# The first weight matrix of a two-layer encoder, loaded raw and split on the engines chunk by chunk

## The chip, the cores and the metric

The kernel runs on one core of one Trainium2 chip. The metric is device time in microseconds (us) for one execution of the whole program. Engines are named as in the profile: PE is TensorE (PEld its weight loads), DVE is VectorE, ACT is ScalarE, POOL is GpSimd, SP is SyncE.

## The reference

Two layers of an encoder work on x of 512 tokens by 1024 features, all in float32. Each layer does

```
h = rms_norm(x, attn_norm_g[l]);  z = h @ w_in[l]
qa, ka, va, qb, kb, vb, ga, gb = split(z)          # 512,128,128,512,512,512,1024,1024 columns
ya = window_gqa(rope(norm(qa)), rope(norm(ka)), va, sink_a[l]) @ w_proj_a[l]
yb = neighbourhood_attn(norm(qb), norm(kb), vb, rel_bias_b[l]) @ w_proj_b[l]
x = x + (sigmoid(ga) * ya + sigmoid(gb) * yb) @ w_out[l]
h = rms_norm(x, ffn_norm_g[l])
x = x + (silu(h @ w_gate[l]) * (h @ w_up[l])) @ w_down[l]
```

The case is about the very first product, the 512 columns of qa in layer 0.

## The kernel before

**Precision.** A float32 product is made of three products in the faster float32r format: each operand is split into a high part (its rounding to float32r) and a low part (what is left). For a weight the high part H is a transfer that rounds on its way, and the low part L is made by `w_low`: ScalarE writes -H, and an accumulating transfer adds the weight from memory a second time. Both transfers are issued by GpSimd, and the second has to wait for ScalarE.

**Slabs.** Weights come in slabs. The first matrix (columns of qa) has four slabs of 256 rows by 512 columns, 512 KB each; a slab holds two chunks of 128 rows. `w_load(i)` issues the transfer of H of slab i, `w_low(i)` makes L, and `w_take` hands them to the product. For later slabs both are issued at due times ahead of their use.

**The first product.** `token_matmul` keeps four PSUM banks, one for each block of 128 tokens. For each of eight chunks k it does twelve products of 128 by 512: for each block xh·H, xh·L, xl·H. In layer 0 the chunks of x are prepared on the way by `start(nrm, k, second)`: PE transposes the chunk `xin[k]` in four blocks, ACT writes its high part `xh` with the norm's gain, DVE copies the transposed chunk to `xT`, then DVE makes the low part `xl`, ACT squares the chunk, and DVE adds the squares up in `acc`. Two chunks are prepared ahead of the first product, the other six between products. After the eighth chunk four small products with `ones` sum the squares over the features, DVE computes the reciprocal root (`rstd`) in some sixteen tiny operations, and PE turns it into rows; only then does the program's next matrix (columns of ka and va) begin.

**The order.** PE's main line is written out in code order. Everything beside it (the rope tables in `chain_tables`, heads, splits) stands in generators, and a dry run with a planner's costs decides once, at build time, between which products their instructions go. On the chip each engine then runs its list in that order. Buffers lie in two arenas (float32 and float32r), and a packer gives them addresses from the uses in the dry run.

**Small loads.** SP issues x in eight chunks, the identity matrix and the norm gains `vec`. POOL issues the first three slabs, the rest of the constants, four loads of norm vectors, `posi`, two loads `gqa`, and the sinks `snk`. A transfer may have to wait for an earlier one of its kind: GpSimd's ninth waits until its first has landed.

Of the kernel before, what the change touches and what calls it, by code (L numbers as in the profile page):

```python
# [12 lines left out]
F32 = mybir.dt.float32  # L13
F32R = mybir.dt.float32r
I32 = mybir.dt.int32
AF = mybir.ActivationFunctionType
ALU = mybir.AluOpType
AX = mybir.AxisListType

P = 128  # L20
# [4 lines left out]
NB = S // P  # L25
KD = D // P
# [64 lines left out]
def by_columns(ap):  # L91

    return ap.rearrange("p (r cc c) -> p cc r c", cc=NB, r=8)


def held(ap):
    return ap.rearrange("p (cc r c) -> p cc r c", cc=NB, r=8)
# [116 lines left out]
def trunk(ctx: ExitStack, tc: tile.TileContext, a: dict, out: bass.AP, lay: Layout):  # L214
    nc = tc.nc
    PS = bass.MemoryType.PSUM
    cp = ctx.enter_context(tc.tile_pool(name="cp", bufs=1))
# [37 lines left out]
    def at_bank():  # L255
        return pa.tile([P, S], F32, tag="at", name=nm("at"))
# [76 lines left out]
    T = Engine(nc.tensor, "pe")  # L333
# [167 lines left out]

    highs, lows, used = {}, {}, [0]

    def w_load(i):

        if i not in highs:
            n1, n2, src = plan[i]
            highs[i] = buf([n1, n2], F32R)
            for at, ap in src:
                n = ap.shape[1]  # L510
                GQ.dma_start(highs[i][:, :, at : at + n], ap.rearrange("(k p) n -> p k n", p=P))

    def w_low(i):

        if i not in lows:
            n1, n2, src = plan[i]
            lows[i] = buf([n1, n2], F32R)
            A.activation(lows[i], highs[i].bitcast(F32), AF.Copy, scale=-1.0)
            for at, ap in src:
                n = ap.shape[1]  # L520
                GQ.dma_start(
                    lows[i][:, :, at : at + n], ap.rearrange("(k p) n -> p k n", p=P), accum_op=ALU.add
                )
# [110 lines left out]
    G.memset(vec2, 0.0)  # L634
    G.memset(ones, 1.0)
    G.memset(magic, 0x5F3759DF)
    warm = cp.tile([P, 2], F32, tag="warm", name="warm")
    A.copy(warm, ones)
    xv = a["x"].rearrange("o (b p) d -> p (o b) d", p=P)
    xin = []  # L640

    def x_load(c):
        t = act().rearrange("p (b n) -> p b n", b=NB)
        Q.dma_start(t, xv[:, :, P * c : P * c + P])
        xin.append(t)


    x_load(0)
    Q.dma_start(ident, a["consts"][:, :P])
    for i, n in enumerate(("attn_norm_g", "ffn_norm_g")):  # L650
        Q.dma_start(vec[16 * i : 16 * i + 16], a[n].rearrange("l (k p) -> (l k) p", p=P))
    w_load(0)
    for c in range(1, KD):
        x_load(c)
        if c in (3, 5):
            w_load((0, 3, 5).index(c))
    GQ.dma_start(cst[:, P:], a["consts"][:, P:])
    for i, n in enumerate(("q_norm_b", "k_norm_b")):
        for h in range(2):
# [7 lines left out]
        GQ.dma_start(gqa[:, i], a[n].rearrange("l d -> (l d)").unsqueeze(0).to_broadcast([P, DEPTH * HD]))  # L667
    snk = cp.tile([P, DEPTH, 8], F32, tag="snk", name="snk")
    GQ.dma_start(snk, a["sink_a"].rearrange("l h -> (l h)").unsqueeze(0).to_broadcast([P, DEPTH * 8]))
    ps = at_bank()  # L670
    T.transpose(ps[:, :32], vec, ident[:32, :32])
    V.tensor_copy(vecT, ps[:, :32])

    def gain(norm, k):
        c = 16 * (norm % 2) + 8 * (norm // 2) + k
        return vecT[:, c : c + 1]
# [140 lines left out]
    def token_matmul(nrm, evac, begin=None):  # L817

        ps = [mm_bank() for _ in range(NB)]
        if begin is not None:  # L820
            begin(0, False)
            w_low(0)
            begin(0, True)
            begin(1, False)
            begin(1, True)
            tick(0.0)
        for k0 in range(0, KD, 2):
            wk = w_take()
            order = [(b, k) for b in range(NB) for k in range(2)]
            if begin is not None:  # L830
                order.sort(key=lambda x: x[1])
            for i, (b, k) in enumerate(order):
                t = slice(P * b, P * b + P)
                kk = k0 + k
                hi, lo = wk[k]
                mm(ps[b], nrm.xh[kk][:, t], hi, kk == 0, False)
                mm(ps[b], nrm.xh[kk][:, t], lo, False, False)
                mm(ps[b], nrm.xl[kk][:, t], hi, False, kk == KD - 1)
                tick(UNIT)
                if kk == KD - 1:  # L840
                    evac(b, ps[b])
                if begin is not None and i in (0, 2, 4, 6) and k0 < KD - 2:
                    begin(k0 + 2 + i // 4, i % 4 == 2)
                yield UNIT


# [219 lines left out]

    norms = {}

    def start(nrm, k, second):

        if not second:
            ps = at_bank()
            for b in range(NB):
                T.transpose(ps[:, P * b : P * b + P], xin[k][:, b, :], ident)
            A.activation(held(nrm.xh[k]), by_columns(ps), AF.Copy, scale=gain(0, k))
            V.tensor_copy(held(xT[k]), by_columns(ps))
            return
        V.scalar_tensor_tensor(nrm.xl[k], xT[k], gain(0, k), nrm.xh[k].bitcast(F32), ALU.mult, ALU.subtract)
        sq = act()
        A.activation(sq, xT[k], AF.Square)  # L1080
        if nrm.acc is not None:
            V.tensor_tensor(sq, sq, nrm.acc, ALU.add)
        nrm.acc = sq
        if k == KD - 1:
            done.add("acc0")
# [507 lines left out]
```

## Time and profile before

| | us |
|---|---|
| median of 3 runs | 1441.97 |
| lowest and highest of them | 1440.86, 1449.07 |
| the profiled execution | 1444.73 |
| its span (first to last instruction) | 1442.9 |
| PE busy, in the span | 1394.6 (97%) |
| DVE busy | 912.2 (63%) |
| ACT busy | 706.8 (49%) |
| POOL busy (its transfer issues count) | 363.4 (25%) |

In rows of the timeline the first number is the start and the second the duration, both in us; behind them stand engine, line, operation, what it writes and reads, and in brackets how long the engine sat idle ahead of it and for whom. Line 308 is the helper that records every operation, so rows are told apart by names and shapes: `mm` and `at` are PSUM banks, `arena` all buffers of the two arenas. The profiled execution is 1.83 us longer than its span.

### The profile page before, as it was taken

The page shows a single profiled execution, that of the slowest core. Times are in us where ns is not written, and L with a number is a line of the kernel's source. Part 1 is how long each engine was busy: PE and PEld are TensorE (multiplying, and loading weights), DVE is VectorE, ACT ScalarE, POOL GpSimd, SP SyncE. Part 2 cuts the span into 40 slices and gives each one's busy share as a digit, 9 for nine tenths or more (in the row PEclk, how much of TensorE's full clock was granted, in tenths as well). Part 3 has the DMA queues.
Part 4 walks back from the last instruction along what each step waited for, and adds up shares of the span by engine and source line. Part 5 has one row for each costly group of instructions (what it writes and reads, how often), then busy time and mean ns, then how long its engine had stood idle before and what let it go on. Part 6 is the DMA issues. An engine that isn't in the chain of part 4 may idle for free.

```text
span 1442.9 us, 20988 instructions
## 1 busy us (share of the span) xinstructions
PE 1394.6 (97%) x8074; PEld 1224.6 (85%) x8074; DVE 912.2 (63%) x1752; ACT 706.8 (49%) x1191; POOL 363.4 (25%) x370
## 2 busy tenths in 40 slices
PE   5999999999989999999999999999998999999998
PEld 3778888888779999999987788888887999999997
DVE  3977777543667565665648768783448666574753
ACT  3476766643454343433544776574346343343431
POOL 4533222233221111101244322223232120111110
PEclk9999999999999999999999999999998999999999
DMA  9977788799865645645699678888996674736555
GB/s 226 170 159 129 140 161 157 142 196 259 146 139 144 156 117 143 155 112 117 134 201 174 132 129 155 160 158 155 260 206 109 147 175 116 178 89 145 121 100 117
DMA packets 209316, 221.10 MB, mean 153 GB/s; under 512 B 25900, under 2 KB 177632, under 8 KB 209216
## 3 DMA queue, kind: packets, MB, share of 16 engines
q0 software_dynamic: 157808, 165.13, 61.3%
q1 hardware_dynamic: 51408, 54.62, 13.3%
q8 instruction: 64, 1.05, 0.3%
q14 instruction: 36, 0.29, 0.1%
HBM read 207.13 MB, written 2.10 MB: 145 GB/s over the span
## 4 chain that ended last, share of the span: by engine, by line
PE 77%; DVE 12%; issue 3%; DMA 3%; ACT 3%; POOL 1%; DVEq 0%; POOLq 0%; ACTq 0%
PE mm L308 60%; PE at L308 18%; DVE arena L308 9%; ACT arena L308 3%; DVE sm L308 3%; DMA arena<-in_w_in 2%; DMA arena<-in_w_up 1%; POOL arena L308 1%; DMA cst<-in_consts 1%; DVE hf L308 0%; DVE den L308 0%; ACT L308 0%; ACT mm L308 0%; ACT sm L308 0%; DVEq L308 0%
## 5 line engine op out<-in xcount | busy, mean ns | idle before, releaser
L308 PE MATMUL mm<-arena 128*128 128x512 f32 (+1 forms) x5568 | 1123.6, 357 | 20.7 <-ACT mm L308 12.5
L308 PEld LDWEIGHTS mm<-arena 128*128 128x128 f32 x5568 | 907.1, 191 | 150.3 <-ACT mm L308 12.9
L308 ACT ACTIVATE arena<-arena 128x1024 fp32r<-128x1024 f32 (+3 forms) x276 | 232.7, 862 | 188.8 <-DMA arena<-in_w_down 58.9
L308 ACT CAST arena<-arena 128x1024 fp32r<-128x1024 f32 (+2 forms) x250 | 212.0, 864 | 220.9 <-DVE arena L308 218.5
L308 PE MATMUL at<-arena 128*128 128x256 f32 (+2 forms) x1952 | 303.8, 296 | 5.0 <-DVE arena L308 3.5
L308 PEld LDWEIGHTS at<-arena 128*128 128x128 f32 x1952 | 265.7, 191 | 25.9 <-DVE arena L308 8.1
L308 DVE TENSOR_TENSOR arena<-arena,arena 128x1024 fp32r<-128x1024 f32 (+2 forms) x240 | 233.0, 984 | 59.7 <-ACT arena L308 59.3
L308 DVE TENSOR_TENSOR arena<-arena,mm 128x512 f32<-128x512 f32 x144 | 98.7, 686 | 248.4 <-PE mm L308 248.3
L308 POOL DMA_DIRECT2D arena<-in_w_in x168 | 168.3, 1368 | 339.3 <-ACT arena L308 329.5
L308 POOL DMA_DIRECT2D arena<-in_w_down x96 | 98.2, 1218 | 502.1 <-ACT arena L308 357.5
L308 DVE TENSOR_TENSOR arena<-arena 128x1024 f32<-128x1024 f32 (+3 forms) x196 | 158.3, 823 | 4.0 <-ACT arena L308 1.5
L308 DVE TENSOR_TENSOR arena<-at,arena 128x384 fp32r<-128x384 f32 (+4 forms) x206 | 114.4, 562 | 49.6 <-ACT arena L308 42.2
L308 ACT CAST arena<-at 128x384 fp32r<-128x384 f32 (+2 forms) x164 | 74.4, 459 | 117.2 <-PE at L308 99.9
L308 PE MATMUL at<-cst,arena 128*128 128x128 f32 x504 | 85.9, 277 | 9.7 <-DVE arena L308 5.7
L308 PEld LDWEIGHTS at<-cst,arena 128*128 128x128 f32 x504 | 64.3, 142 | 26.8 <-DVE arena L308 6.8
L308 ACT ACTIVATE arena<-arena,negm 128x256 f32<-128x256 f32 (+1 forms) x128 | 71.4, 559 | 6.5 <-DVE negm L308 5.7
L308 DVE TENSOR_TENSOR arena<-mm,arena 128x512 f32<-128x512 f32 x72 | 49.3, 686 | 33.7 <-PE mm L308 33.6
L308 ACT COPY arena<-at 64x512 f32<-64x512 f32 (+1 forms) x60 | 34.9, 582 | 69.8 <-PE at L308 68.5
L308 POOL DMA_DIRECT2D arena<-in_w_out x32 | 35.1, 1287 | 60.5 <-ACT arena L308 60.5
L308 DVE CUSTOM_DVE_ANT_0 arena<-at,cst,nsnk 128x256 f32<-128x256 f32 (+1 forms) x64 | 34.4, 546 | 18.0 <-PE at L308 17.7
L308 DVE CUSTOM_DVE_ANT_0 arena<-at,arena 128x256 f32<-128x256 f32 (+1 forms) x64 | 30.7, 484 | 15.0 <-PE at L308 14.6
L308 DVE TENSOR_SCALAR arena<-arena,sm 128x384 f32<-128x384 f32 (+1 forms) x102 | 33.9, 387 | 1.1
(70 smaller groups left out, 436.4 us busy)
## 6 DMA issues: line engine op xcount, KB each, us to landing
arena<-in_w_in POOLq DMA_DIRECT2D x104, 512.0 KB, 7.2
arena<-in_w_down POOLq DMA_DIRECT2D x80, 512.0 KB, 6.7
arena<-in_w_gate SPq DMA_DIRECT2D x20, 1024.0 KB, 7.5
arena<-in_w_up SPq DMA_DIRECT2D x20, 1024.0 KB, 5.3
arena<-in_w_in POOLq DMA_DIRECT2D x64, 256.0 KB, 6.3
arena<-in_w_out POOLq DMA_DIRECT2D x32, 512.0 KB, 8.4
arena<-in_w_proj_a POOLq DMA_DIRECT2D x16, 512.0 KB, 7.0
arena<-in_w_proj_b POOLq DMA_DIRECT2D x16, 512.0 KB, 5.9
```

What stands on the lines that cost most here:

```text
L308: f(*args, **kw)
```

## The change

The first matrix isn't loaded as rounded high parts any more. `first_load(i)` brings each of its four slabs as plain float32 into a new buffer `raws[i]`: slab 0 in two halves of 256 KB by ACT's queue, slabs 1 to 3 by POOL's. `first_parts(k)` makes the parts of chunk k: ACT casts to the high part, DVE subtracts for the low part. `start(nrm, k)` now does all of a chunk in one go, `first_parts` first, and the copy to `xT` goes from DVE to ACT. One chunk is prepared ahead of the first product instead of two; each further chunk is prepared behind the first three products of the chunk before. The two gain loads go to ACT's queue, ahead of the half slabs; the identity is SP's first load, then x. The `warm` operation, which brings the first table load with it, stands behind the loads.

```
+    def first_load(i):
+        n1, n2, ((_, ap),) = plan[i]
+        raws[i] = buf([n1, n2])
+        ap = ap.rearrange("(k p) n -> p k n", p=P)
+        if i:
+            GQ.dma_start(raws[i], ap)
+        else:
+            for k in range(2):
+                AQ.dma_start(raws[i][:, k], ap[:, k])
+        highs[i], lows[i] = buf([n1, n2], F32R), buf([n1, n2], F32R)
+    def first_parts(k):
+        raw, h, lo = raws[k // 2][:, k % 2], highs[k // 2][:, k % 2], lows[k // 2][:, k % 2]
+        A.copy(h, raw)
+        V.tensor_tensor(lo, raw, h.bitcast(F32), ALU.subtract)
...
-    x_load(0)
     Q.dma_start(ident, a["consts"][:, :P])
...
-        Q.dma_start(vec[16 * i : 16 * i + 16], a[n].rearrange("l (k p) -> (l k) p", p=P))
-    w_load(0)
-    for c in range(1, KD):
+        AQ.dma_start(vec[16 * i : 16 * i + 16], a[n].rearrange("l (k p) -> (l k) p", p=P))
+    for c in range(KD):
         x_load(c)
-        if c in (3, 5):
-            w_load((0, 3, 5).index(c))
+        if c % 2 == 0:
+            first_load(c // 2)
...
         if begin is not None:
-            begin(0, False)
-            w_low(0)
-            begin(0, True)
-            begin(1, False)
-            begin(1, True)
+            begin(0)
             tick(0.0)
...
-                if begin is not None and i in (0, 2, 4, 6) and k0 < KD - 2:
-                    begin(k0 + 2 + i // 4, i % 4 == 2)
+                if begin is not None and b == 0 and kk + 1 < KD:
+                    begin(kk + 1)
...
-    def start(nrm, k, second):
+    def start(nrm, k):
+        first_parts(k)
...
-            V.tensor_copy(held(xT[k]), by_columns(ps))
+        A.copy(held(xT[k]), by_columns(ps))
```

Since the dry run sees other costs at the start, the planner also puts the rope tables elsewhere. Behind the first matrix's part of the program the engines' lists are the same instructions in the same order as before, but for a few rows; buffers have other addresses, and some of the later waits name another engine.

Three places show it. The first is ScalarE in the second half of the first product. Before, around the table load (`trig` are the rope tables, the row of 128x1024 is the -H of a later slab, 128x512 into arena_73 from `at` is xh, 128x512 within arena_72 is the square):

```order
L308 ACTIVATE arena_72<-arena_72 128x512
L308 ACTIVATE arena_73<-at_257,vecT 128x512
L308 ACTIVATE arena_73<-arena_73 128x1024
L308 ACTIVATE arena_72<-arena_72 128x512
L308 ACTIVATE arena_73<-at_287,vecT 128x512
L308 ACT_TABLE_LOAD
L308 ACTIVATE trig<-arena_72 128x128
L308 ACTIVATE arena_72<-arena_72 128x512
L308 ACTIVATE trig<-arena_72 128x128
```

And now, from the -H ahead of chunk 4 to the -H behind chunk 5:

```order
L308 ACTIVATE arena_73<-arena_73 128x1024
L308 CAST arena_73<-arena_72 128x512
L308 ACTIVATE arena_73<-at_232,vecT 128x512
L308 COPY arena_72<-at_232 128x512
L308 ACTIVATE arena_72<-arena_72 128x512
L308 ACT_TABLE_LOAD
L308 ACTIVATE trig<-arena_72 128x128
L308 CAST arena_73<-arena_72 128x512
L308 ACTIVATE arena_73<-at_264,vecT 128x512
L308 COPY arena_72<-at_264 128x512
L308 ACTIVATE arena_72<-arena_72 128x512
L308 ACTIVATE arena_73<-arena_73 128x1024
```

A chunk now has four operations of ScalarE where it had two, and the table load with a `trig` stands between two chunks, ahead of the cast that the next chunk's first products need.

The second place is VectorE, where `chain_tables` begins. Before, it stood behind the copy of chunk 5:

```order
L308 COPY arena_72<-at_223 128x512
L308 CAST vec_76<-posi 4x128
L308 TENSOR_SCALAR nsnk<-snk 128x16
L308 SCALAR_TENSOR_TENSOR arena_73<-arena_72,vecT,arena_73 128x512
L308 TENSOR_TENSOR arena_72<-arena_72 128x512
```

Now it stands behind the sum of squares of chunk 1, ahead of both low parts of chunk 2 (the row with two sources is the weight's, the one with `vecT` is xl):

```order
L308 TENSOR_TENSOR arena_72<-arena_72 128x512
L308 CAST vec_76<-posi 4x128
L308 TENSOR_SCALAR nsnk<-snk 128x16
L308 TENSOR_TENSOR arena_73<-arena_72,arena_73 128x512
L308 SCALAR_TENSOR_TENSOR arena_73<-arena_72,vecT,arena_73 128x512
```

The two small rows that need the loads `posi` and `snk` moved from chunk 5 to chunk 2.

The third place is PE at the end of the first product. Before:

```order
L308 MATMUL mm_120<-arena_73 128x512 x3
L308 MATMUL at_337<-ones,arena_72 128x1 x4
L308 MATMUL mm_121<-arena_73 128x512 x3
L308 MATMUL mm_118<-arena_73 128x512 x3
L308 MATMUL mm_119<-arena_73 128x512 x3
L308 MATMUL mm_120<-arena_73 128x512 x3
L308 MATMUL mm_121<-arena_73 128x512 x3
L308 MATMUL at_389<-cst,rstd_344 128x128 x4
```

And now, with `mm_120` the first block of tokens:

```order
L308 MATMUL mm_120<-arena_73 128x512 x3
L308 MATMUL at_359<-ones,arena_72 128x1 x4
L308 MATMUL mm_121<-arena_73 128x512 x3
L308 MATMUL mm_122<-arena_73 128x512 x3
L308 MATMUL mm_123<-arena_73 128x512 x3
L308 MATMUL at_400<-cst,rstd_366 128x128 x4
```

Between the sums of squares and the turning of `rstd` there stood fifteen products of 128x512, and now nine.

More of the change, by code (lines that the diff above doesn't have):

```diff
@@ L502, in trunk @@
     highs, lows, used = {}, {}, [0]
+    FIRST = KD // 2
+    raws = {}
+    def first_load(i):
[12 more added lines that the diff above has]
+        V.tensor_tensor(lo, raw, h.bitcast(F32), ALU.subtract)
     def w_load(i):
@@ L636, in trunk @@
     G.memset(magic, 0x5F3759DF)
-    warm = cp.tile([P, 2], F32, tag="warm", name="warm")
-    A.copy(warm, ones)
     xv = a["x"].rearrange("o (b p) d -> p (o b) d", p=P)
@@ L669, in trunk @@
     GQ.dma_start(snk, a["sink_a"].rearrange("l h -> (l h)").unsqueeze(0).to_broadcast([P, DEPTH * 8]))
+    warm = cp.tile([P, 2], F32, tag="warm", name="warm")
+    A.copy(warm, ones)
     ps = at_bank()
@@ L1067, in trunk @@
     norms = {}
-    def start(nrm, k, second):
[L1071 to L1075, printed above, removed]
-            V.tensor_copy(held(xT[k]), by_columns(ps))
-            return
+    def start(nrm, k):
+        first_parts(k)
+        ps = at_bank()
+        for b in range(NB):
+            T.transpose(ps[:, P * b : P * b + P], xin[k][:, b, :], ident)
+        A.activation(held(nrm.xh[k]), by_columns(ps), AF.Copy, scale=gain(0, k))
+        A.copy(held(xT[k]), by_columns(ps))
         V.scalar_tensor_tensor(nrm.xl[k], xT[k], gain(0, k), nrm.xh[k].bitcast(F32), ALU.mult, ALU.subtract)
```

## The prediction

> **What bounds the kernel now.** I read the busy shares first, then who PE waits for over the whole span, then PE's timeline at the start.
>
> ```profile
> PE 1394.6 (97%) x8074; PEld 1224.6 (85%) x8074; DVE 912.2 (63%) x1752; ACT 706.8 (49%) x1191; POOL 363.4 (25%) x370
> PE mm L308 <- ACT mm L308: 12.5, 2, 6.3
> PE mm L308 <- DMA arena<-in_w_in: 8.3, 1, 8.3
> PE at L308 <- DMA vec<-in_ffn_norm_g: 5.8, 1, 5.8
> PE at L308 <- DMA arena<-in_x: 3.9, 1, 3.9
> ```
>
> PE is busy 97% of the time; 18.0 us of its waits (8.3, 5.8, 3.9) are for transfers, each once. All three lie in the first 21 us:
>
> ```profile
> 11.78 0.78 PE L308 MATMUL mm<-arena 128*128 128x512 f32 x1
> 20.83 1.22 PE L308 MATMUL mm<-arena 128*128 128x512 f32 x2 [8.28 <-DMA arena<-in_w_in]
> 21.84 1.06 PE L308 MATMUL at<-cst,arena 128*128 128x128 f32 x4
> 26.65 3.00 PE L308 MATMUL mm<-arena 128*128 128x512 f32 x12
> 29.85 3.01 PE L308 MATMUL mm<-arena 128*128 128x512 f32 x12
> 49.18 0.65 PE L308 MATMUL at<-cst,rstd 128*128 128x128 f32 x4 [0.54 <-DVE rstd L308]
> 49.59 11.87 PE L308 MATMUL mm<-arena 128*128 128x512 f32 x51
> ```
>
> One product runs at 11.78, its weight's high part being there. The second needs the low part and starts at 20.83. From then to 49.18 PE stands still for 0.54 us only. So every us by which the stream begins earlier is a us of the end, unless something in it runs dry. The chain of waits agrees at this place:
>
> ```profile
> 12.56 8.23 DMA arena<-in_w_in
> ```
>
> The accumulating transfer is issued at 12.56, behind the small loads in GpSimd's queue, and lands at 20.79.
>
> **Term 1: the first weights.** The accumulating transfer goes. In its place stand a plain half slab (third on ScalarE's queue) and the operations that split it. I place its issue like the third on SyncE's queue before, at 1.78. Rows with an engine have the start of issue first; rows with KB end with the time from issue to landing, and the row of three numbers is such a time too, of chunk 1 of x:
>
> ```profile
> 1.78 0.42 SPq L308 DMA_DIRECT2D vec<-in_attn_norm_g  x1
> vec<-in_attn_norm_g SPq DMA_DIRECT2D x1, 8.0 KB, 3.6
> arena<-in_x SPq DMA_DIRECT2D x1, 256.0 KB, 3.0
> 2.72 9.79 SPq L308 DMA_DIRECT2D arena<-in_x  x7
> DMA to landing us min/median/max: 8.2/8.2/8.2
> 1.35 2.30 POOL L308 DMA_DIRECT2D arena<-in_w_in  x3 [0.31 <-issue]
> arena<-in_w_in POOLq DMA_DIRECT2D x1, 512.0 KB, 5.5
> ```
>
> The first row is where the third issue stands; it lands after 3.6. Chunk 0 of x, with the engines still empty, takes 3.0; chunk 1, the same 256 KB issued at 2.72 beside GpSimd's slabs, 8.2; GpSimd's first slab, issued at 1.35, 5.5, landed at 6.9. Bounds for the half slab: 1.78 + 3.0 = 4.8 and 1.78 + 8.2 = 10.0. I take 7.0, by the slab: same rows of the same matrix, first big load of its queue. Then chunk 0 goes through these durations:
>
> ```profile
> L308 ACT CAST arena<-arena 128x512 fp32r<-128x512 f32 x76 | 46.9, 619 | 84.9 <-DVE arena L308 84.8
> L308 ACT ACTIVATE arena<-at,vecT 128x512 fp32r<-128x512 f32 x8 | 5.5, 688 | 19.4 <-PE at L308 19.4
> L308 ACT COPY arena<-at 128x512 f32<-128x512 f32 x28 | 16.2, 579 | 50.1 <-PE at L308 50.1
> L308 DVE SCALAR_TENSOR_TENSOR arena<-arena,vecT,arena 128x512 fp32r<-128x512 f32 x8 | 6.0, 749 | 0.2
> L308 DVE TENSOR_TENSOR arena<-arena,arena 128x512 fp32r<-128x512 f32 x76 | 52.1, 688 | 24.1 <-ACT arena L308 23.9
> ```
>
> Cast 0.62, xh 0.69, copy 0.58, xl 0.75: 2.64, with hops about 2.8, so the third product starts at 9.8 and ends at 10.2; the weight's low part (0.69 on DVE) is hidden under xh and the copy. The same point before is 21.84. **Term 1: -11.6.** DVE loses a copy of 0.69 a chunk and gains a subtraction of 0.69, which is nothing. PE makes one chunk's transposes more inside the stream: a product takes 11.87 / 51 = 0.23, and from 26.65 to 29.85 there are twelve and a chunk's transposes, which leaves **+0.45**. The transfers lose 2 MB, the second reading. What is late next is x's chunk 1, which landed at 10.9 (2.72 + 8.2) and would then be 0.7 behind the third product; I count it at nothing, since no gain load stands ahead of it any more.
>
> **Term 2: VectorE waits for `snk`.** The load used to be long there; its reader moved from chunk 5 to chunk 2.
>
> ```profile
> 12.02 0.53 POOL L308 DMA_DIRECT2D snk<-in_sink_a  x1 [0.45 <-DMA cst<-in_consts]
> snk<-in_sink_a POOLq DMA_DIRECT2D x1, 8.0 KB, 5.0
> 35.09 0.17 DVE L308 TENSOR_SCALAR nsnk<-snk 128x16 f32<-128x16 f32 x1
> ```
>
> It landed at 17.0 and GpSimd's queue ahead of it is unchanged. Behind it DVE has the weight's low part and xl of chunk 2 (0.17 + 0.69 + 0.75, hops 0.15), and PE waits for xl. By the rows above, PE gets from the third product of chunk 0 to that of chunk 2 in 29.65 - 21.84 = 7.8 us: at 18.0. With snk at 17.0 it is 18.75 plus the product. Three queues now share the engines where it was two, so I take 17.5: **+1.5**; bounds 0 (landed by 16) and 3 (at 19).
>
> **Term 3: ScalarE in chunks 4 to 6.** A chunk costs it 0.62 + 0.69 + 0.58 + 0.62 (square) = 2.5 us, and PE 29.85 - 26.65 = 3.2. That leaves 0.7. The square's row and the extra work between chunks:
>
> ```profile
> L308 ACT ACTIVATE arena<-arena 128x512 f32<-128x512 f32 x102 | 60.3, 622 | 36.3 <-DVE arena L308 36.2
> L308 ACT ACTIVATE arena<-arena 128x1024 fp32r<-128x1024 f32 x158 | 166.9, 1057 | 150.4 <-DMA arena<-in_w_down 56.8 <-DMA arena<-in_w_out 44.9 <-DMA arena<-in_w_in 13.0
> 40.60 1.28 ACT L308 ACT_TABLE_LOAD   x1
> 42.02 0.31 ACT L308 ACTIVATE trig<-arena 128x128 f32<-128x128 f32 x1
> 41.51 1.13 DVE L308 TENSOR_SCALAR arena<-arena 128x128 f32<-128x128 f32 x5
> 43.82 0.94 DVE L308 SCALAR_TENSOR_TENSOR arena<-arena 128x128 f32<-128x128 f32 x3
> 44.79 0.23 DVE L308 TENSOR_SCALAR arena<-arena 128x128 f32<-128x128 f32 x1
> ```
>
> Ahead of chunk 4 stands a -H (1.06); ahead of chunk 5 the table load and a `trig` (1.59), which waits for the chunk's sum of squares (0.69) and five DVE rows (1.13), 1.8 after the square and so 0.55 past the load; ahead of chunk 6 a -H and a `trig` (1.37), which waits for 0.69 + 0.94 + 0.23, 0.8 past the -H. So 1.06, 2.15 and 2.15 against a slack of 0.7 and another 0.35 between xl and its product: 0 + 1.1 + 1.1. **+2.2**; bounds 0 and 4.5 (slack 0 and late low parts on DVE). The queue behind these waits is ScalarE's next cast, whose high part PE needs first.
>
> The Trainium skill, "ScalarE: Activation LUTs", section "What ACT_TABLE_LOAD costs", gives a load 1.283 us and a drain of 1.38 beside it. The load's row has 1.28, and `trig` starts 0.14 behind it. By the page, with a drain ahead of the load, the sum would be some 1.4 worse; the row decides.
>
> **Term 4: the end of the product.** Between the sums with `ones` and the turning of rstd stood fifteen products, now nine:
>
> ```profile
> 45.88 0.15 DVE L308 TENSOR_SCALAR sm<-at 128x4 f32<-128x4 f32 x1
> 48.96 0.16 DVE L308 SCALAR_TENSOR_TENSOR rstd<-sm,sm 128x4 f32<-128x4 f32 x1
> ```
>
> DVE needs 3.24 from sm to rstd, with hops 3.4; nine products cover 2.1 of it, so PE waits 1.3 in place of 0.54, +0.8. The sums wait for the chunk's addition of squares on DVE, 0.69 behind xl, under which PE has one product of 0.23: +0.45. **+1.2**; bounds 0.5 and 2.
>
> **Term 5: behind it.** Six operations of the rope tables move from behind rstd to ahead of it, so DVE starts its next chain about 1.3 us earlier against PE. PE's later waits for it:
>
> ```profile
> PE at L308 <- DVE arena L308: 2.0, 4, 0.8
> ```
>
> That is between 60 and 130 us. I take **-0.3**, bounds -1.3 and 0. The rest of the lists is as before, and PE is covered there as it was.
>
> **Sum:** -11.6 + 0.45 + 1.5 + 2.2 + 1.2 - 0.3 = -6.55. The profiled execution, 1444.73 with 1.83 outside its span, would be 1438.2; it lies 2.8 above the median of the runs, 1441.97, from which I get 1435.4.
>
> **The rivals.** *The half slab is shared out* and lands at 10.0. For it:
>
> ```profile
> q0 software_dynamic: 205, 0.39, 124.2%
> q1 hardware_dynamic: 9, 0.00, 1.7%
> ```
>
> Between 5 and 6 us GpSimd's queue moved 205 packets and SyncE's 9, and chunk 1 of x took 8.2. Against it: SyncE's queue held two gain loads ahead of chunk 1, the first landing at 5.4 (1.78 + 3.6), and x may have waited behind them, not beside the slabs. It costs 3.0, less the 1.5 of term 2, which then hides: 1436.9. The Trainium skill, "DMA: Bandwidth & Descriptors", section "Issuing engines are not separate DMA queues", says loads issued by several engines interleave on the same sixteen engines and save issue time only. By that rule this rival is the likelier; the 9 packets lean to it, the row of chunk 0 does not reach so far.
>
> *All goes well*: half slab at 5.0, snk by 14 (an earlier start needs it earlier), terms 2 and 3 together 0.5 in place of 3.7. That is 2.0 + 3.2 better: 1430.2.
>
> *The gain is given back, and more*: the four raw buffers put 4,096 words more into the float32 arena during the start, so the packer gives later buffers other neighbours, and w_gate or w_up loads in the feed-forward part wait for a reader that is done later. PE's two waits of 6.3 for ACT above are of that kind (a seed copy late at the head of that part). A wait as long in each layer again would cost 12.5: 1447.9, slower by 0.4%. It decides from 6.55 on. Against it: the instruction lists behind the start are the same.
>
> *Nothing comes of it*: ScalarE's -H of the next matrix stands late (ahead of chunk 4), GpSimd's queue waits for it in order, and PE waits at the second matrix for all it has won: 1442. Against it: by my terms that -H is done at about 23, its transfer, at 8.2 like the one of before, at 31, and the need is at 42.
>
> **How the numbers follow.** Forecast 0.55, shared out 0.22, all well 0.12, given back 0.06, nothing 0.05. The range reaches from all well to the bad bounds of the unknown costs: half slab at 10.0 (+1.5 net), term 3 at 4.5 (+2.3) and term 4 at 2 (+0.8), 1440.0. About 1% is what a measurement of this kernel can tell from no change, here 14.4 us; the start holds only 20.8 us and PE needs the operations of chunk 0 in any case, so faster by over 1% needs every bound at its best (0.04), slower by over 1% two such mishaps as the third (0.03).
>
> **What would show it.** PE's first product at about 8.4 and its third at 9.8; DVE waiting for snk's transfer until about 17.5; two PE waits of about 1 us at chunks 5 and 6 with ScalarE ahead of them; a wait of 1.3 for rstd, whose turning starts at about 42.9 where it was 49.18; and from there every row 6 to 7 us earlier to the end. Wrong would be: a first product behind 11; a distance at rstd that shrinks or grows later; a wait of PE for weights of the second matrix.

## The result: 0.57% faster, and the profile after

The changed kernel takes 1436.04 us (median of 8 runs, 1434.55 to 1437.91), the kernel before 1444.42 us on the same chip (8 runs, 1440.86 to 1449.07). The ratio is 0.9943, with a 95% interval of 0.9927 to 0.996, so the change saves between 5.8 and 10.5 us. That is within 1%, as forecast, but on the faster side beyond doubt. The median of before was 1441.97 in the first 3 of its runs, on which the forecast stands, and is 2.45 higher in all 8. The profiled execution took 1437.88 with a span of 1436.1; before it was 1444.73 and 1442.9.

The busy shares of the changed kernel, and who PE waits for over the whole span (total, times, longest). One large row is left out here: 12.1 for DVE in sixteen waits, all of them behind the first product (11.5 in fifteen before).

```profile
PE 1396.5 (97%) x8074; PEld 1224.4 (85%) x8074; DVE 913.5 (64%) x1752; ACT 710.3 (49%) x1203; POOL 358.3 (25%) x365
PE mm L308 <- ACT mm L308: 11.2, 2, 6.2
PE at L308 <- DMA vec<-in_ffn_norm_g: 4.0, 1, 4.0
PE mm L308 <- ACT arena L308: 3.1, 2, 2.7
PE mm L308 <- DVE arena L308: 2.0, 4, 1.1
PE at L308 <- DVE rstd L308: 1.3, 1, 1.3
```

The wait of 8.3 for the weights' transfer is gone, and so is that of 3.9 for x. PE now waits for the engines that make the parts: 3.1 for ACT, 2.0 and 1.3 for DVE. PE's busy time is much as it was (1394.6 before).

PE's timeline during the first product, with the rows left out in which the products of a chunk run on. The four transposes of 128x128 mark where each chunk begins to be prepared, from chunk 1 to chunk 7:

```profile
8.20 2.06 PE L308 MATMUL mm<-arena 128*128 128x512 f32 x3 [2.66 <-ACT arena L308]
10.05 1.05 PE L308 MATMUL at<-cst,arena 128*128 128x128 f32 x4
...
14.73 0.60 PE L308 MATMUL at<-cst,arena 128*128 128x128 f32 x4
...
18.85 0.50 PE L308 MATMUL mm<-arena 128*128 128x512 f32 x1 [1.08 <-DVE arena L308]
...
19.85 0.60 PE L308 MATMUL at<-cst,arena 128*128 128x128 f32 x4
...
23.06 0.60 PE L308 MATMUL at<-cst,arena 128*128 128x128 f32 x4
...
26.34 0.60 PE L308 MATMUL at<-cst,arena 128*128 128x128 f32 x4
...
29.70 0.50 PE L308 MATMUL mm<-arena 128*128 128x512 f32 x1 [0.23 <-DVE arena L308]
30.04 0.60 PE L308 MATMUL at<-cst,arena 128*128 128x128 f32 x4
...
33.13 0.78 PE L308 MATMUL mm<-arena 128*128 128x512 f32 x2 [0.40 <-ACT arena L308]
34.40 0.50 PE L308 MATMUL mm<-arena 128*128 128x512 f32 x1 [0.48 <-DVE arena L308]
34.73 0.60 PE L308 MATMUL at<-cst,arena 128*128 128x128 f32 x4
...
38.18 1.02 PE L308 MATMUL at<-ones,arena 128*128 128x1 f32 x8
...
42.67 0.62 PE L308 MATMUL at<-cst,rstd 128*128 128x128 f32 x4 [1.32 <-DVE rstd L308]
```

The row of the turning of rstd, 49.18 before, stands at 42.67: 6.51 earlier. The end of the span is 6.8 earlier. So in these two executions practically all of the gain is made in this first product, and the end still has it.

The distances between these rows are the best ledger of the product, better than the times in brackets: a wait that PE has inside a group of products is not in a bracket, and after each wait the product's own row is longer too (0.50 for one, where twelve take 3.02). A chunk without a wait takes 23.06 - 19.85 = 3.21. The others take 4.68, 5.12, 3.28, 3.70, 4.69 and, up to the sums with ones, 3.45. In the first of them, 4.68, PE has no wait: its products start 0.43 apart until 13.2 and 0.23 apart from there on, and at 13.2 the trace's records of the granted clock begin, with 1.00. Before, the same change of pace comes at 24.5. The same rows of before that the prediction does not show:

```profile
26.30 0.60 PE L308 MATMUL at<-cst,arena 128*128 128x128 f32 x4
...
32.70 0.60 PE L308 MATMUL at<-cst,arena 128*128 128x128 f32 x4
...
36.04 0.60 PE L308 MATMUL at<-cst,arena 128*128 128x128 f32 x4
...
39.25 0.60 PE L308 MATMUL at<-cst,arena 128*128 128x128 f32 x4
44.05 1.02 PE L308 MATMUL at<-ones,arena 128*128 128x1 f32 x8
```

From 21.84, where three products are done, to the sums and on to 49.18 the stream of before took 27.34. The changed one takes 32.62 from 10.05, at the same state of the products. The stream starts 11.79 earlier and loses 5.28 of it on the way.

ScalarE and VectorE at the places that the prediction named:

```profile
6.94 0.62 ACT L308 CAST arena<-arena 128x512 fp32r<-128x512 f32 x1 [2.67 <-DMA arena<-in_w_in]
25.55 1.28 ACT L308 ACT_TABLE_LOAD   x1
26.98 0.31 ACT L308 ACTIVATE trig<-arena 128x128 f32<-128x128 f32 x1
31.67 0.31 ACT L308 ACTIVATE trig<-arena 128x128 f32<-128x128 f32 x1 [1.20 <-DVE arena L308]
18.02 0.17 DVE L308 TENSOR_SCALAR nsnk<-snk 128x16 f32<-128x16 f32 x1 [3.71 <-DMA snk<-in_sink_a]
```

The first cast starts when the half slab is there, at 6.9; DVE stands still for 3.71 until snk is there, at 18.0; the second trig waits 1.20 for DVE.

### The profile page after: what moved, and what is told of

It reads as the page before. It is cut to its first block, busy times and chain, and to the rows that moved or that the text cites. A ratio compares the mean times of both kernels' runs of the same rounds, so it can differ in the third digit from the quotient of the medians.

```text
span 1436.1 us, 21014 instructions
## 1 busy us (share of the span) xinstructions
PE 1396.5 (97%) x8074; PEld 1224.4 (85%) x8074; DVE 913.5 (64%) x1752; ACT 710.3 (49%) x1203; POOL 358.3 (25%) x365
## 4 chain that ended last, share of the span: by engine, by line
PE 72%; DVE 14%; issue 5%; ACT 4%; DMA 3%; POOL 2%; DVEq 0%; POOLq 0%; ACTq 0%
PE mm L308 54%; PE at L308 18%; DVE arena L308 10%; ACT arena L308 4%; DVE sm L308 3%; POOL arena L308 2%; DMA arena<-in_w_up 1%; DMA cst<-in_consts 1%; DMA arena<-in_w_out 1%; DMA arena<-in_w_in 0%; DMA snk<-in_sink_a 0%; DVE hf L308 0%; DVE den L308 0%; ACT mm L308 0%; ACT sm L308 0%
## 5 line engine op out<-in xcount | busy, mean ns | idle before, releaser
L308 PE MATMUL mm<-arena 128*128 128x512 f32 (+1 forms) x5568 | 1126.4, 357 | 16.3 <-ACT mm L308 11.2
L308 PEld LDWEIGHTS mm<-arena 128*128 128x128 f32 x5568 | 907.7, 191 | 148.8 <-ACT mm L308 11.6
L308 ACT CAST arena<-arena 128x1024 fp32r<-128x1024 f32 (+2 forms) x258 | 216.8, 856 | 220.4 <-DVE arena L308 214.5
L308 ACT ACTIVATE arena<-arena 128x1024 fp32r<-128x1024 f32 (+3 forms) x272 | 228.4, 859 | 192.2 <-DMA arena<-in_w_down 66.8
L308 DVE TENSOR_TENSOR arena<-arena,arena 128x1024 fp32r<-128x1024 f32 (+2 forms) x248 | 238.6, 975 | 66.1 <-ACT arena L308 65.7
L308 POOL DMA_DIRECT2D arena<-in_w_in x163 | 163.1, 1372 | 337.1 <-ACT arena L308 319.2
L308 ACT COPY arena<-at 128x512 f32<-128x512 f32 (+1 forms) x68 | 39.5, 581 | 68.0 <-PE at L308 66.8
```

The source lines that it names most:

```text
L308: f(*args, **kw)
```

## The experiments

The variants differ by one to two microseconds, and the interval of a timed comparison is two on either side. So each verdict rests on the start of a row in the profile, above all the turning of rstd, and the times only say that nothing is lost later. A single profile has its own chance: in the three with the changed kernel's list of loads and of operations up to chunk 3 (the changed kernel, no_sine, trig_without_wait) the first cast stands at 6.94, 7.30 and 6.86, the first product at 8.20, 8.56 and 8.12, and the chunk behind it, with its slow products, takes 4.68, 5.33 and 4.23. Differences of half a us at the start, and of a us at rstd where no later wait evens them out, say little. Each run has the kernel before beside it on the same chip (medians 1442.98, 1443.43 and 1443.31 in the three timed comparisons).

**pool_slab0: is it the half slab on a queue of its own that starts the stream?** Slab 0 goes as one load of 512 KB on GpSimd's queue, like the others.

```
-        if i:
-            GQ.dma_start(raws[i], ap)
-        else:
-            for k in range(2):
-                AQ.dma_start(raws[i][:, k], ap[:, k])
+        GQ.dma_start(raws[i], ap)
```

> Slab 0 too is loaded raw by GpSimd's queue, as one load of 512 KB ahead of the other three; all else as in the changed kernel. Theory A (the gain is the earlier start of PE's product stream, less what runs dry in it): in the kernel before, GpSimd's first slab landed at 6.9, where the half slab lands now, so PE's first product stays at 8 to 8.5 us. Every load behind it in GpSimd's queue comes 1.5 to 2 us later, so snk lands near 19.7 instead of 18.0 and PE's row for rstd moves from 42.7 to 44 to 44.5; time +1.5 against the changed kernel. Rival B (ScalarE's queue is what brings the gain): first product behind 10, rstd row behind 45, time +3 or more.

```profile
9.30 2.06 PE L308 MATMUL mm<-arena 128*128 128x512 f32 x3 [3.78 <-ACT arena L308]
```

The first cast stands at 8.04 and the turning of rstd at 44.04 (42.67 in the changed kernel). The first product, 9.30, lies between the two forecasts; rstd is where theory A put it. The half slab by ScalarE's queue is worth 0.7 to 1.2 us at the start, so it is a part of the gain and not the gain. Time 1436.8, ratio to before 0.9964 (0.9946 to 0.9982).

**snk_first: what does VectorE's wait cost?** GpSimd's queue begins with the loads of snk and posi, ahead of the slabs.

```
+    GQ.dma_start(snk, ...)
+    GQ.dma_start(posi[64:68], ...)
     Q.dma_start(ident, a["consts"][:, :P])
```

> The changed kernel with the small loads of snk and posi issued first on GpSimd's queue, ahead of the three raw slabs. The engines' lists are otherwise the same. Theory A with its term 2: VectorE's wait of 3.7 us for snk and PE's waits of 1.1 and 0.2 at chunk 2 go, and PE gets from the third product of chunk 0 to that of chunk 2 in 7.8 us, so its transposes behind chunk 2's first block start at 18.0 to 18.3 instead of 19.85, the rstd row at 41.0 to 41.3 instead of 42.67, and the time falls by 1.5. Rival D (the wait only hides another one: the raw slab 1 or x, pushed back by two small loads): the wait stays at 0.8 or more and the rstd row at 42 or later.

```profile
14.46 0.17 DVE L308 TENSOR_SCALAR nsnk<-snk 128x16 f32<-128x16 f32 x1
41.29 0.62 PE L308 MATMUL at<-cst,rstd 128*128 128x128 f32 x4 [1.26 <-DVE rstd L308]
```

DVE no longer waits for snk, PE's two waits for DVE in chunk 2 are gone, and rstd turns 1.38 earlier although the first product came 0.49 later (8.69). Not all of these 1.9 us are the wait's: the chunk with the slow products took 4.13, not 4.68, by chance. Chunk 2 takes 3.83 where it took 5.12, and 0.34 of that is a new wait of PE ahead of the transposition of the norm vectors. In half_slab_first, half_slab_then_gains and slabs_behind below, where snk is early too and that wait isn't there, chunk 2 takes 3.31 to 3.34. So the wait for snk cost 1.8. Time 1435.17, ratio 0.9953 (0.994 to 0.9965). The span, 1432.3, is the shortest of all profiles here, but of the 3.8 us to the changed kernel's only 1.4 are made by rstd.

**slab0_raw_only: is the first slab all that matters?** Only slab 0 is loaded raw; slabs 1 to 3 come as high parts with an accumulating transfer, as before.

```
-        elif c % 2 == 0: first_load(c // 2)
+        elif c % 2 == 0: w_load(c // 2)
-        first_parts(k)
+        if k < 2: first_parts(k)
```

> Only slab 0 is loaded raw and split on the engines; slabs 1 to 3 are loaded as rounded high parts and get their low parts by accumulating transfers as before. Rival C (all that counts is the first slab): the start as now, rstd row at 42.7 or earlier, since ScalarE and VectorE have less to do. Theory A: the accumulating transfer of slab 1 cannot be issued before GpSimd is through with snk, near 13, and lands 8 us later, near 21 to 23, where chunk 2 needs it at 15; PE waits there for 3 us or more, and the rstd row stands at 44.5 to 46.5, so about half of the gain of 6.5 is left.

```profile
20.91 0.74 PE L308 MATMUL mm<-arena 128*128 128x512 f32 x2 [1.88 <-DMA arena<-in_w_in]
44.76 0.62 PE L308 MATMUL at<-cst,rstd 128*128 128x128 f32 x4 [1.67 <-DVE rstd L308]
```

PE waits for the low part of the second slab, 1.88 and not 3 or more, and two of the 6.5 us are lost: rival C is out. Of the two, 0.8 are lost at the start (first product 9.00). Behind the wait the granted clock is 0.50 from 22 to 25, and the next chunk takes 4.79. Time 1436.9, ratio 0.9958 (0.9945 to 0.9972).

**before_low_first: the kernel before with its first accumulating transfer issued early.** The low part of slab 0 is issued directly behind GpSimd's three slab loads, ahead of the small loads.

```
         if c in (3, 5):
             w_load((0, 3, 5).index(c))
+    w_low(0)
```

> The kernel before, with one edit: the accumulating transfer of slab 0 is issued directly behind the first three slabs, ahead of the constants and the eight small loads. It has to wait for ScalarE's -H, near 8. Theory A: it lands near 14 to 16 instead of 20.8, PE's stream starts there, and the rstd row moves from 49.18 to 44 to 46: most of the gain is the place in GpSimd's queue, not the engine that makes the low part. Rival E (an accumulating transfer is slow whatever its place, or the small loads are then late): start at 18 or later, rstd row at 47 or later.

```profile
16.74 1.22 PE L308 MATMUL mm<-arena 128*128 128x512 f32 x2 [4.39 <-DMA arena<-in_w_in]
51.60 0.65 PE L308 MATMUL at<-cst,rstd 128*128 128x128 f32 x4 [0.68 <-DVE rstd L308]
18.53 4.04 POOL L308 DMA_DIRECT2D arena<-in_w_in  x4
27.64 1.58 ACT L308 ACTIVATE arena<-arena 128x1024 fp32r<-128x1024 f32 x2 [8.10 <-DMA arena<-in_w_in]
```

A miss for theory A, and a useful one. The stream starts 4.1 earlier (20.83 before), at 16.74 and not at 14 to 16, yet rstd turns 2.4 later, at 51.60, as rival E had it (47 or later). GpSimd's queue waits 4.26 for the early transfer's operand and later 4.06 until a load of the weights has landed, and issues the last slab's high part and the other accumulating transfers only from 18.53 on (15.49 before); ScalarE then stands still for 8.10. Ratio 0.9999 (0.9983 to 1.0016). So an early start alone isn't the gain: taken with slab0_raw_only, the change holds what it wins because no accumulating transfer is left in this stage.

**copy_by_dve: the copy to xT back on VectorE.**

```
-        A.copy(held(xT[k]), by_columns(ps))
+        V.tensor_copy(held(xT[k]), by_columns(ps))
```

> The changed kernel with one line back: the copy to xT is made by VectorE again, so ScalarE has three operations a chunk (1.9 us) and VectorE four (0.69 + 0.69 + 0.75 + 0.69 = 2.8 us) against PE's 3.2 us. Theory A, the move of the copy is what keeps the product dense: VectorE also has some 8 us of rope tables to do during the product, and with a slack of 0.4 us a chunk it becomes late; PE waits for VectorE in several chunks, and the turning of rstd, 42.67 in the changed kernel, comes at 44 to 47. Theory B, ScalarE bounds the chunks 4 to 6: the waits of 0.40 and 0.48 there go and nothing comes in their place; rstd turns at 41.7 to 42.3.

```profile
37.48 0.50 PE L308 MATMUL mm<-arena 128*128 128x512 f32 x1 [0.76 <-DVE arena L308]
46.49 0.62 PE L308 MATMUL at<-cst,rstd 128*128 128x128 f32 x4 [1.27 <-DVE rstd L308]
```

Chunk 0 comes 0.3 earlier, then PE waits for DVE in five of the eight chunks, and rstd turns 3.8 later: theory A. Time 1440.15 in one run. Without this part of the change over half of the gain at rstd is gone: with the copy VectorE is the later of the two engines, and ScalarE has the room for it. What ScalarE alone costs PE in chunks 4 to 6 this run can't say, since VectorE's waits lie over it.

**no_sine: is it the table load?** The two trig operations make a square, not a sine, so that no table is loaded there.

```
-            A.activation(trig[:, i], r, AF.Sin)
+            A.activation(trig[:, i], r, AF.Square)
```

> The two trig operations compute a square in place of a sine (the rope tables are left wrong), so that the table load of 1.28 us between chunks 4 and 5 isn't there, and the one back ahead of the exponentials neither; all else is the same row for row. The prediction charged 1.1 us of PE to chunk 5 because of this load. Theory A, the load lies in ScalarE's slack by now: chunk 5's wait (0.23) is for VectorE's low part and stays, the waits of chunk 6 are for VectorE's row ahead of the second trig and stay; the turning of rstd comes at 42.3 to 42.7. Theory B, the load does push the later chunks as the prediction reckoned: rstd turns 0.8 to 1.2 earlier, at 41.5 to 41.9.

```profile
27.02 0.31 ACT L308 ACTIVATE trig<-arena 128x128 f32<-128x128 f32 x1 [1.46 <-DVE arena L308]
42.71 0.62 PE L308 MATMUL at<-cst,rstd 128*128 128x128 f32 x4 [1.28 <-DVE rstd L308]
```

Without the load the trig starts at 27.02; with it, at 26.98. The 1.28 of the load are now 1.46 of waiting for DVE, and rstd turns where it did (42.67). Taking away the load alone wins nothing here, since the wait for DVE ends at the same moment.

**trig_without_wait: is it the wait for VectorE?** The same, and the trig operations read the angles, which are ready early; VectorE makes all its rows, but their result goes unused.

```
-            A.activation(trig[:, i], r, AF.Sin)
+            A.activation(trig[:, i], ang, AF.Square)
```

> As no_sine, and the two trig operations square the angles themselves, which VectorE has ready before chunk 3, so that ScalarE waits for nothing there; VectorE makes all its rows of the rope tables as before, but their result goes unused (the rope tables are left wrong). In no_sine and in the changed kernel the first trig starts at 27.0 with or without the table load ahead of it, and the second 1.2 behind the -H ahead of it, when VectorE's row is done; from the transposes of chunk 4 to those of chunk 7 PE takes 2.0 more than for chunks without waits (3.7 and 4.7 for chunks 5 and 6, not 3.2). Theory A, it is ScalarE's next cast queued behind a trig that waits for VectorE: chunks 5 and 6 then take 3.2 to 3.5 and the turning of rstd comes at 41.0 to 41.8 (42.71 in no_sine, if chunk 0 comes as it did there). Theory B, VectorE's own rows between the low parts are what is late: chunks 5 and 6 stay at 3.7 and 4.7, rstd at 42.5 to 42.9.

```profile
23.57 0.60 PE L308 MATMUL at<-cst,arena 128*128 128x128 f32 x4
...
26.85 0.60 PE L308 MATMUL at<-cst,arena 128*128 128x128 f32 x4
...
30.06 0.60 PE L308 MATMUL at<-cst,arena 128*128 128x128 f32 x4
...
34.20 0.60 PE L308 MATMUL at<-cst,arena 128*128 128x128 f32 x4
```

Chunks 4, 5 and 6 take 3.28, 3.21 and 4.14 where the changed kernel takes 3.28, 3.70 and 4.69. Half of the loss, 1.04 of 2.04, was ScalarE's cast standing behind a trig that came late. In chunk 5 (0.49) the trig stands behind the table load and behind the wait for VectorE, which end together, and this run has neither; which of the two would do alone was not run. In chunk 6 (0.55) there is no load, and the wait for VectorE is the cause. The other half, 0.93, stays in chunk 6, and PE's waits there (0.23 and 0.17) are for VectorE's two low parts, ahead of which VectorE works through 2.6 us of table rows without a gap. No run took those rows away, so for them the cause is read from the trace alone. Both theories are half right. (rstd turns at 42.15, since snk came 0.5 later here: PE's wait in chunk 2 ends at 19.36, not 18.85.)

**Four runs on who comes first to the engines.** The half slab took 5.3 from issue to landing, close to what the prediction took from a row; was it held up by the slabs beside it? First the gain loads on SyncE's queue, so that the half slab is issued at 0.74 and x later (on top of snk_first):

```
-        AQ.dma_start(vec[16 * i : 16 * i + 16], ...)
+        Q.dma_start(vec[16 * i : 16 * i + 16], ...)
```

> As snk_first (GpSimd's queue begins with the loads of snk and posi), and besides the two gain loads go from ScalarE's queue to SyncE's, behind the identity, so that the first half slab is issued at 0.74 and not at 1.66, while x starts some 0.9 later. Theory A, the half slab has its own time of 5.3 to 5.8 from issue to landing: it lands at 6.0 to 6.5, PE's first product comes at 7.3 to 7.8 (8.69 in snk_first), and the turning of rstd at 40.2 to 40.8 (41.29 in snk_first), if chunk 0 of x and the gains are not later than it. Theory B, the landing is set by what all queues together bring in the first us (the half slab's packets alternate with those of the slabs and of x): it lands at 6.8 to 7.4 as before, and rstd turns at 41.2 to 42. Median of the timed runs in A 1433.5 to 1435, in B as snk_first.

```profile
3.82 0.62 ACT L308 CAST arena<-arena 128x512 fp32r<-128x512 f32 x1 [0.66 <-DMA arena<-in_w_in]
8.91 1.12 PE L308 MATMUL at<-cst,arena 128*128 128x128 f32 x4 [2.92 <-DMA arena<-in_x]
```

Neither theory foresaw this. The half slab lands after 3.1 and its cast starts at 3.82, three us early. But chunk 0 of x, which stands ahead of it in the changed kernel (issued at 1.20 there, landed by 4.4), is now behind it, is issued at 2.12, behind the gains, and lands at 8.9. The first product comes at 10.80 and rstd turns at 43.40. Time 1435.81, ratio 0.9951 (0.9937 to 0.9966).

Then the changed kernel with GpSimd's small loads and constants ahead of the raw slabs 1 to 3 (slabs_late):

```
-        if c % 2 == 0:
-            first_load(c // 2)
+        if c == 0:
+            first_load(0)
...
+    for i in range(1, FIRST):        # behind the small loads
+        first_load(i)
```

> The changed kernel with GpSimd's queue turned round: all its small loads first, the raw slabs 1 to 3 behind them, issued from about 6 us on and not from 1.3. During the first 6 us the half slab then shares the engines with x and small loads alone. Theory A, the rival of the prediction (the half slab is shared out among the queues): it lands at 5 to 6 where it landed at 6.9, PE's first product comes at 6.3 to 7.5 and not at 8.20. Theory B, the half slab's 5.3 us are not set by the slabs beside it: first product at 8.0 to 8.4. In both snk is there early, VectorE doesn't wait in chunk 2, and slab 1 lands at 12 to 14; rstd turns at 39.5 to 40.8 in A, at 41.2 to 41.6 in B, later if slab 1 isn't there for chunk 2.

```profile
6.72 0.62 ACT L308 CAST arena<-arena 128x512 fp32r<-128x512 f32 x1 [2.46 <-DMA arena<-in_w_in]
41.53 0.62 PE L308 MATMUL at<-cst,rstd 128*128 128x128 f32 x4 [1.23 <-DVE rstd L308]
```

The half slab lands only 0.2 earlier, less than the 0.9 by which profiles with the same order of loads differ (6.39 in copy_by_dve, 7.30 in no_sine). This does not tell the theories apart as cleanly as I meant: the constants (328 KB) took the slabs' place, and GpSimd's queue moved 0.16 MB between 3 and 4 us and 0.18 MB in the next. rstd turns 1.1 earlier, as snk is early, though slab 1 now lands only at 15.8 (12 to 14 expected) and chunk 2 takes 4.18. Time 1435.58, ratio 0.9944 (0.9929 to 0.9959).

So the half slab was put first and x left where it was, the gain loads between the two half slabs (on top of snk_first):

```
+            AQ.dma_start(raws[i][:, 0], ap[:, 0])
+            for j, n in enumerate(("attn_norm_g", "ffn_norm_g")):
+                AQ.dma_start(vec[16 * j : 16 * j + 16], ...)
+            AQ.dma_start(raws[i][:, 1], ap[:, 1])
```

> As snk_first, and on ScalarE's queue the first half slab is issued ahead of the two gain loads (at 0.74, not at 1.66), the second half behind them. SyncE's queue is as in the changed kernel, so x starts where it did. In half_slab_first the half slab landed 3.1 us behind its issue, but chunk 0 of x, issued 0.9 later, landed only 6 to 7 us behind its own. Theory A, one transfer at a time gets the engines and the later one pays: with the half slab at 0.74 and chunk 0 of x at about 1.2 the one of them that is later lands at 6 to 8, PE's first product stays at 7.5 to 9 and the turning of rstd at 40.3 to 41.5. Theory B, the engines share evenly and the order hardly matters: both land at about 5.5, first product at 7.0, rstd at 39.6 to 40. If the gain loads, now behind the half slab, land last, PE's first transposition (4.05 in the changed kernel) is at 5 to 6.

```profile
7.26 0.28 PE L308 MATMUL at<-cst,vec 32*128 32x32 f32 x1 [7.26 <-DMA vec<-in_ffn_norm_g]
```

The half slab lands 3.1 behind its issue, chunk 0 of x 3.5 behind its own, at 4.7. Now a gain load of 8 KB, issued at 1.65, takes 5.5 and is the last; the first product comes at 9.36 and rstd turns at 42.30. Both theories miss: neither of the two big loads is late, and the gain comes over a us later than foreseen. Time 1434.51, ratio 0.9942 (0.9927 to 0.9957).

Last the same with the constants and slabs 1 to 3 late on GpSimd's queue, snk, posi and the four small vectors ahead of them:

```
+    GQ.dma_start(snk, ...)
+    GQ.dma_start(posi[64:68], ...)
     ...                              # the four loads of vec2
+    for i in range(1, FIRST):
+        first_load(i)
+    GQ.dma_start(cst[:, P:], a["consts"][:, P:])
```

> As half_slab_then_gains, and on GpSimd's queue the loads of snk, posi and the four small vectors stand ahead of the raw slabs 1 to 3, and the constants behind them; slab 1 is issued some 3 us later than in snk_first. Theory A, the slabs beside it are what delays the later of the half slab and chunk 0 of x: both land by 5 to 5.5, first product at 6.2 to 7.0, rstd at 39.0 to 39.8, slab 1 (landing at 10 to 11.5) is there for chunk 2. Theory B, the half slab and x delay each other and the gain loads, whatever GpSimd does: first product as in half_slab_then_gains within 0.5, rstd at 40 to 41.5. Median of the timed runs 1432.5 to 1435 in A, as snk_first (1435.2) in B.

The queues between 5 and 6 us in this run (packets, MB, share), q1 being SyncE's with x, q10 ScalarE's and q0 GpSimd's:

```profile
q1 hardware_dynamic: 254, 0.13, 66.6%
q10 hardware_dynamic: 20, 0.01, 4.2%
q0 software_dynamic: 14, 0.00, 1.5%
```

The gain load still lands only at 7.28, the first product comes at 9.38, as theory B has it; rstd turns at 41.75, 0.25 beyond its range. Time 1435.84, ratio 0.9951 (0.9937 to 0.9966). GpSimd moves next to nothing here and the gain load is no earlier; ScalarE's queue gets 20 packets through beside SyncE's 254. So in this order it is the half slab, x and the gains that hold each other up. Each order that was tried has one of them early and another late. The order of the changed kernel (gains, x, half slab) has the earliest first product, 8.69 in snk_first, on which the others are built, against 10.80 (x last) and 9.36 (a gain last). Its last load is no earlier than the gain (the cast stands at 7.43 in snk_first, the gain's reader at 7.26), but fewer operations stand between the half slab and the first product.

## Why the prediction was right

Forecast 1435.4 and -6.55; measured 1436.04, and between the profiled executions -6.85. The medians beside each other on one chip differ by 8.4 (5.8 to 10.5), so that the forecast time is hit to 0.6 us is in part luck: the median it started from lies 2.45 below that of the 8 runs. What can be checked closely is the start. The ledger of the first product closes: -11.79 + 0.36 + 0.22 + 1.78 + 2.04 + 0.86 = -6.53, against the -6.51 at rstd. Term by term:

- **Term 1, the first weights** (-11.6 and +0.45): -11.79 and +0.36. First product 8.20 (forecast 8.4), the transposes behind the third at 10.05 (10.2). One chunk's transposes cost 0.36 in the stream. The half slab landed at 6.9, taken as 7.0; in other profiles with this order of loads the cast stands between 6.39 (copy_by_dve) and 7.30 (no_sine), so a hit to 0.1 is chance. The bound of 4.8 proved real too: issued first, such a load takes 3.1 to 3.2.
- **x's chunk 1, counted at nothing**: rightly, PE has no wait ahead of its transposes at 10.05.
- **The slow products of the start**, which the prediction doesn't have: the chunk before the wait for snk takes 4.68, the first one of before 26.30 - 21.84 = 4.46. That is +0.22, since the change of pace comes 3.1 us into this chunk now and came 2.6 into it before. Its size is chance: the same chunk takes 4.23 in trig_without_wait and 5.33 in no_sine, and the wait for snk behind it evens most of that out.
- **Term 2, snk** (+1.5): it landed at 18.0, not 17.5. Chunk 2 takes 5.12 - 3.21 = 1.91 too long, before it was 36.04 - 32.70 = 3.34, so +1.78. The three runs below snk_first with snk early and no other wait there (3.31 to 3.34) confirm the size.
- **Term 3, ScalarE in chunks 4 to 6** (+2.2): 0.07 + 0.49 + 1.48 = +2.04. The size is right; of the mechanism half is shown. The prediction charged chunks 5 and 6 alike, 1.1 us of PE each, to ScalarE's next cast standing behind a `trig` that waits for VectorE. That the cast stands there is right, and it is worth 1.04 in all (trig_without_wait), 0.49 and 0.55, not 2.2. The first `trig` came 0.15 behind the table load, not 0.55; the second waited 1.20 behind the -H, not 0.8. The step that failed is that VectorE's low parts were taken to be in time: they stand only in the bad bound of 4.5 and in no term of the sum, and ahead of chunk 6 they cost the remaining 0.93, by PE's waits there. That a charge of twice the size and a term left out gave the right sum is luck.
- **Term 4, the end** (+1.2): the wait for rstd is 1.32, forecast 1.3. The +0.45 for the sums with ones was mis-sized: a product takes (3.21 - 0.36) / 12 = 0.2375 here; from the last transposes to the sums it is 3.45, 0.24 above a chunk, and before it was 44.05 - 39.25 = 4.80 with six products more, 0.17 above. From the sums to rstd it is 4.49, and before 5.13 less six products, 3.70. That makes 0.07 + 0.79 = +0.86.
- **Term 5, behind it** (-0.3): not seen; the sign is rather the other. PE's waits for DVE in the same part of the program are 2.5 (53.5 to 123.5 us) where they were 2.0, and the distance to before, 6.51 at rstd, is 6.02 at the 200th matmul.

The rivals. *The half slab shared out* at 10.0 didn't happen: 6.9. The Trainium skill, "DMA: Bandwidth & Descriptors", section "Issuing engines are not separate DMA queues", says that loads of several engines interleave on the same sixteen; the four last runs agree that they do, since what one load gains by being first another loses. But which is first mattered by 2 to 3 us for a load (3.1 or 5.3 for the half slab), and the rule alone, by which the prediction called this rival the likelier while it gave it 0.22, gave the wrong landing. *All goes well* needed the half slab at 5.0, snk by 14 and terms 2 and 3 small. half_slab_first and half_slab_then_gains have the half slab by 4 and no wait for snk, but x or a gain is late there, and chunks 4 to 6 cost what they did. *The gain given back* at the head of the feed-forward part: PE's two long waits for ACT are there as before (6.3 before, 6.2 now), and no longer. The distance to before is 6.3 us at the 500th matmul, 6.7 at the 1000th, 8.2 from the 2000th to the 3000th and 6.7 at the last, so nothing builds up by layers. It does not stand still either, which the prediction named as a sign of being wrong: ahead of the feed-forward sums of the first layer PE waits 0.59 for DVE now and 2.34 before, ahead of those of the second 1.87 now, with the halved clock of the last section behind it. No run tells whether the change has a part in these. *Nothing comes of it*: PE has no wait for weights of the second matrix.

On the table load the row decided rightly: it begins at 25.55, directly behind the square that ends at 25.52. The drain of 1.38 that the Trainium skill, "ScalarE: Activation LUTs", section "What ACT_TABLE_LOAD costs", adds to it is not to be seen in this trace: `trig` starts at 26.98, 0.15 behind the load's end.

## What to carry to other kernels

Where a tuned kernel waits once at its start for a prepared operand, loading it raw and preparing it on engines that stand idle can win most of that wait, but look in the same place for what must now be ready sooner: here a small load at the end of a queue, 1.8 of the 5.3 us lost. Take every prepared load of the stage off the queue, not the first alone; the early start of one moved the wait to the next. And measure a dense stream by the distance between rows that repeat, since the idle times in brackets showed only about half of what the stream lost in chunks 5 and 6 (1.11 of 1.97).

## What the runs showed that I had not expected

A wait of PE costs more than its length. At the head of the feed-forward part PE waits 6.2 for ACT; here are PE's row behind the wait, and stretches of the changed kernel, with busy time of each engine and, third from the end, the granted clock:

```profile
403.18 5.49 PE L308 MATMUL mm<-arena 128*128 128x256 f32 x24 [6.22 <-ACT mm L308]
396.00:398.00 2.00, 0.96 (x8) 0.75 (x7) 1.97 (x3) 1.95 (x2) 0.72 (x1) 1.00 0.83 123
400.00:402.00 2.00, 0.00 (x0) 0.00 (x0) 1.28 (x3) 1.03 (x2) 1.27 (x1) 0.50 0.72 150
404.00:406.00 2.00, 2.00 (x11) 2.00 (x11) 0.00 (x0) 2.00 (x4) 1.44 (x2) 0.50 1.04 287
410.00:412.00 2.00, 2.00 (x20) 2.00 (x19) 1.73 (x2) 0.23 (x1) 0.00 (x0) 1.00 1.23 193
```

While PE stands still its clock is halved, from 398.9 on, and it stays at 0.50 until about 409, nearly 6 us after PE works again: 11 matmuls in 2 us, not 20. The halved stretch lasted 10.2 us at this place in this execution and 6.8 in that of before, and such stretches come again near 1,080 to 1,115 us. They differ between executions and kernels (6.8 at this place in snk_first), and a few us of the spread of the timed runs can come from them; that was not tried by itself. The Trainium skill, "TensorE: Matmul & The Clock Gate", section "Part 1: The HAM clock gate (the "warmup" mystery)", says that the clock is half after an idle window of about 3.4 us and that the window runs freely; 6.8 and 10.2 are two and three such windows, so the lengths in the traces agree. The condition does not: before, the clock was halved 4.7 us after PE's last product, but in the changed kernel 1.95 us after it (it ends at 396.96), in less than a whole idle window. The two waits for ACT, 12.5 us before and 11.2 now, are, with what follows them, the largest single stalls left in this kernel.
